# Two stages of a one-core kernel take a block of adaptive weights at every step instead of every second one

## The chip, the cores and the metric

The kernel runs on one core of a Trainium2 chip. The metric is the device time of one execution in microseconds (us). Before the change the median of 3 runs is 2345.33 us (2339.2 to 2347.9). The profile is of one execution of 2337.74 us, whose span is 2335.9 us.

## The reference

The model has two blocks over 256 tokens of width 1024. The change lies in the first one. There, for each of two layers, a vector of shifts, scales and gates is computed from the conditioning vector `c`, and it modulates what the mixer and the experts take in and give out:

```python
silu_c = jax.nn.silu(c)
for i in range(DEPTH):                                   # 2 layers
    mod = silu_c @ ada_w[i] + ada_b[i]                   # [1, 1024] @ [1024, 6144]
    sh_t, sc_t, ga_t, sh_c, sc_c, ga_c = jnp.split(mod, N_MOD, axis=-1)
    hn = modulate(rms_norm(x, norm_tm_g[i]), sh_t, sc_t)
    tm = rwkv7_mix(hn, ...) if i == 0 else dilated_attention_mix(hn, ...)
    x = x + ga_t[:, None, :] * tm
    hn = modulate(rms_norm(x, norm_cm_g[i]), sh_c, sc_c)
    x = x + ga_c[:, None, :] * hier_moe(hn, ...)
```

`ada_w` is 2 x 1024 x 6144 floats, 48 MB. Only `sh_t` and `sc_t` of layer 0 are needed before the first mixer, the recurrence (`rwkv7_mix`); the rest is needed after it. The second block (two layers of attention and experts) is not touched.

## The kernel before, in words

The products with `ada_w` are cut into six sections (`Ada.steps`, L1823 on): two layers times three stretches of 2048 columns. A section has 9 steps. Each of the first 8 loads one block of 128 x 2048 floats (1 MB, L78) into a tile `w` and does four matmuls with it (L1840; each shows as two rows in the trace, so a step is 8 rows), one per group of 32 columns of the array, all adding into one PSUM tile. The 9th step works on VectorE: it adds the bias `S` (L1843), for sections with a norm weight `G` scales with it (L1845), and puts the sum as two parts into `R` (L1848, L1850, L1848). `S` and `G` are loaded from the POOL queue (L1828, L1834).

The tiles `w` come from a pool of 4 slots (`nw=4`). `G` takes one of the same slots, and holds it until its section's 9th step has read it. The LoRA weights `lb` take another until the preparation's LoRA matmuls (L893) are done.

Section 0 runs at the start. The other five, 45 steps with 40 blocks, are the generator `side`, and are handed out as filler beside the recurrence's stages:

- `preps(1, ...)`, the second half of the recurrence's preparation (L866 to L950): it builds decays, keys and removal vectors on VectorE, ScalarE and GpSimd, with small matmuls between (L893, L924, L947). It gives 19 turns. `weave` (L581) takes one item of the filler per turn.
- `inverses()` (L993 to L1015): 16 transposes (L1000) bring 16 x 16 blocks to other partitions, 15 rounds of two VectorE instructions (L1006, L1008) invert them, each round needing the one before, and 16 transposes (L1013) bring them back. It gives 16 turns.
- the recurrence itself (L1235): two chains of 8 jobs each, forward and backward, go round in turn with `every(side, 3)`, one step per three rounds.

`every(gen, n)` (L595) takes one step of `gen` and lets n turns go per step. The instructions are then put in order by a list scheduler, so a step's load and its matmuls may stand somewhat before or after the turn that issued them; on each engine they run strictly in that order. After the recurrence comes the output projection with `rw_w_o` (L1257), whose weights go through the same 4 slots.

Of the kernel before, what the change touches and what calls it, by code (L numbers as in the profile page):

```python
# [575 lines left out]
def finish(gen):  # L576
    for _ in gen:
        pass


def weave(main, *fill, rest=True):  # L581

    fill = [iter(f) for f in fill]
    for _ in main:
        while fill:
            try:
                next(fill[0])
                break
            except StopIteration:
                fill.pop(0)  # L590
    for f in fill if rest else ():
        finish(f)


def every(gen, n):  # L595

    for _ in gen:
        for _ in range(n):
            yield
# [104 lines left out]
def rwkv(N, src, I, cst, emit, side, tail, scratch):  # L704
# [5 lines left out]
    def pool(name, bufs=1, st=es, side="right"):  # L710
        return st.enter_context(tc.tile_pool(name=N.nm(name), bufs=bufs, side=side, reuse_waits="tile"))
# [4 lines left out]
    en, e0, e1, e1a = (ExitStack() for _ in range(4))  # L716
# [104 lines left out]
    side = iter(side)  # L821
# [39 lines left out]
    def kknorm(u):  # L861
        sq = [scratch(k).rearrange("p (j t) -> p j t", j=2) for k in range(2)]
        for j in range(4):
            v.tensor_scalar(kn[:, 4 * u + j], kf[:, 4 * u + j], pv[:, 4, 4 * u + j:4 * u + j + 1], -1.0, op0=OP.mult, op1=OP.mult)
        for k in range(2):
            sc.activation(sq[k], kn[:, 4 * u + 2 * k:4 * u + 2 * k + 2], AF.Square)  # L866
        yield
        ps = N.psum("b")
        for j in range(4):
            nc.tensor.matmul(ps[0:8, :T], sel[:, j, :], sq[j // 2][:, j % 2], start=j == 0, stop=j == 3)  # L870
        ri = p2.tile([8, T], F32, tag="ri", name=N.nm("ri"))
        sc.activation(ri, ps[0:8, :T], AF.Sqrt)
        v.tensor_scalar(ri, ri, 1e-12, None, op0=OP.max)
        v.reciprocal(ri, ri)
        yield
        for j2 in range(2):
            ps = N.psum("b")
            for j in range(2):
                nc.tensor.matmul(ps[:, j * T:(j + 1) * T], selT[0:8, 2 * j2 + j, :], ri, start=True, stop=True)
            o = kn[:, 4 * u + 2 * j2:4 * u + 2 * j2 + 2]  # L880
            v.tensor_mul(o, o, ps.rearrange("p (j t) -> p j t", j=2))
        yield
# [69 lines left out]
    def pair(e2, q):  # L952
        live = [prep(z, e2, q) for z in range(2)]
        while live:
            for p in list(live):
                if next(p, live) is live:
                    live.remove(p)
            yield

    def preps(u, q, lag):  # L960
        yield from kknorm(u)
        a, b = pair(2 * u, q2), pair(2 * u + 1, q)
        for _ in range(lag):
            if next(a, b) is b:
                break
            yield
        roundrobin_ = [a, b]
        while roundrobin_:
            for p in list(roundrobin_):
                if next(p, b) is b:  # L970
                    roundrobin_.remove(p)
                yield
# [9 lines left out]
        for z in range(2):  # L982
            X[z] += [ry2.tile([P, 2, 512], F32, name=f"{n}{z}{e}") for e in range(2, 4)]

    weave(preps(1, pool("q3", 2, e0), 1), every(side, 2), rest=False)
    e0.close()
    e2s = ExitStack()
    p2 = pool("p2", 1, e2s)
# [4 lines left out]
    def inverses():  # L993
        g.memset(mcm, 0.0)
        for c in range(16):
            g.memset(mcm[:, c, :, c:c + 1], 1.0)
        for t4 in range(4):
            ps = N.psum("b")
            for t in range(4):
                nc.tensor.transpose(ps[0:64, t * P:(t + 1) * P], nd[:, 4 * t4 + t, :], N.ident)  # L1000
            sc.activation(ncm[:, 4 * t4:4 * t4 + 4].rearrange("p t b i -> p (t b i)"), ps[0:64, :], AF.Copy)
        yield
        for k in range(15, 0, -1):
            n = 16 - k
            tv = tmp[:, 0:n * 8 * k].rearrange("p (c b i) -> p c b i", c=n, b=8)
            v.tensor_mul(tv, ncm[:, k:k + 1, :, 0:k].to_broadcast([64, n, 8, k]),  # L1006
                         mcm[:, k:, :, k:k + 1].to_broadcast([64, n, 8, k]))
            v.tensor_add(mcm[:, k:, :, 0:k], mcm[:, k:, :, 0:k], tv)  # L1008
            yield
        for h in range(2):  # L1010
            ps = N.psum("b")
            for c in range(8):
                nc.tensor.transpose(ps[:, c * 64:(c + 1) * 64], mcm[:, 8 * h + c].rearrange("p b i -> p (b i)"),  # L1013
                                    N.ident[0:64, 0:64])
            sc.activation(m16[:, 8 * h:8 * h + 8], ps.rearrange("p (c x) -> p c x", c=8), AF.Copy)  # L1015
    m16 = pool("m16", 1, eM, "left").tile([P, 16, 64], F32, name="m16")
    weave(inverses(), every(side, 2), rest=False)
    e2s.close()
    en.close()

# [914 lines left out]
class Model:  # L1935
# [3 lines left out]
    def all(self):  # L1939
# [5 lines left out]
        with ExitStack() as es:  # L1945
# [28 lines left out]
            for i in range(2):  # L1974
# [11 lines left out]
                if i == 0:  # L1986
                    def side():
                        for q in range(1, 6):
                            yield from ada.steps(q // 3, q % 3)
                    mixer = rwkv(N, src, I, I["cst_rwkv"], emit, side(), tail, lambda k: half("G", k))  # L1990
                else:
                    mixer = dilated(N, src, I, I["cst_attn"], emit, tail)
# [186 lines left out]
```

## Time and profile before

| | us |
|---|---|
| median of 3 runs | 2345.33 |
| profiled execution | 2337.74, span 2335.9 |
| PE busy | 2038.8 (87% of the span) |
| VectorE (DVE) busy | 1097.0 (47%) |
| preparation, second half | about 180 to 239 |
| inverses (first L1000 to last L1013) | 239.2 to 264.0 |
| recurrence (first L1106 to last L1225) | 264.0 to 458.5 |

PE is TensorE's matmuls, PEld its weight loads, DVE VectorE, ACT ScalarE, POOL GpSimd, SP the queue that issues the loads of `w`. The end of a matmul is modelled, its start is measured, so the distance from start to start is the safer reading. PEclk is the share of full speed that TensorE's clock was granted: 0.50 is 1.2 GHz, 1.00 is 2.4 GHz. The chain that ended last reaches back only over the last 8 us of the program and says nothing of this place, so the stages are read from the timeline of each engine.

### The profile page before, as it was taken

Reading aid. Unit: us, or ns where it says so; the run is one execution under the profiler, and the core shown is the slowest. Engines: PE = TensorE matmul, PEld = TensorE weight load, DVE = VectorE, ACT = ScalarE, POOL = GpSimd, SP = SyncE. Lnnn points to the kernel's source line nnn. Section 1 sums busy time; section 2 is a strip of 40 time slices with the busy share of each in tenths; the row PEclk is TensorE's granted clock in tenths of the full one; section 3 lists DMA queues with packets and bytes.
Section 4 is the critical chain, followed back from the end, with each engine's and each line's share of the span. In section 5 each row is a group of like instructions: output and inputs, shape, how many; then the busy total and the mean of one; then the engine's idle time right before and its main releaser. Section 6 shows DMA issues by size and latency. Waiting matters only on the chain. (4 is left out here: it accounts for less than half of the span.)

```text
span 2335.9 us, 40948 instructions
## 1 busy us (share of the span) xinstructions
PE 2038.8 (87%) x16656; PEld 1459.6 (62%) x16656; DVE 1097.0 (47%) x2437; ACT 679.0 (29%) x1197; POOL 360.6 (15%) x296
## 2 busy tenths in 40 slices
PE   4987899979976999998987799979897799979886
PEld 2864577666543898986643577766563577756552
DVE  4777667663312435364321375562231765642222
ACT  2342133331112344442110245431120345421120
POOL 1144022220000321210000222220010222210010
PEclk7986799989988999999997799989998899989997
DMA  9434643578998553538999644479999443669996
GB/s 278 145 95 147 213 160 102 184 290 336 418 420 340 183 178 101 189 91 339 418 420 419 225 137 134 144 273 379 419 401 410 152 144 127 219 257 412 413 400 267
DMA packets 162999, 605.99 MB, mean 259 GB/s; under 512 B 36961, under 2 KB 37985, under 8 KB 107489
## 3 DMA queue, kind: packets, MB, share of 16 engines
q1 hardware_dynamic: 159072, 599.54, 67.7%
q0 software_dynamic: 3136, 3.16, 0.5%
q8 instruction: 139, 2.28, 0.4%
q14 instruction: 76, 0.61, 0.1%
q10 hardware_dynamic: 576, 0.39, 0.1%
HBM read 601.99 MB, written 1.05 MB: 258 GB/s over the span
## 5 line engine op out<-in xcount | busy, mean ns | idle before, releaser
L360 PE MATMUL psb<-w,xg 128*32 128x256 f32 (+1 forms) x4096 | 394.9, 432 | 87.9 <-DMA w<-in_moe_w_up_dram 27.1
L360 PEld LDWEIGHTS psb<-w,xg 128*32 128x32 f32 (+1 forms) x4096 | 213.4, 135 | 278.5 <-issue 70.7
L561 ACT ACTIVATE wh<-w 128x1024 fp32r<-128x1024 f32 x230 | 240.6, 1060 | 286.4 <-PE psb L651 147.9
L565 POOL TENSOR_TENSOR wl<-w,wh 128x1024 fp32r<-128x1024 f32 x80 | 197.9, 2475 | 577.4 <-ACT wh L561 457.0
L565 DVE TENSOR_TENSOR wl<-w,wh 128x1024 fp32r<-128x1024 f32 x150 | 200.6, 1344 | 166.8 <-ACT wh L561 138.8
L420 DVE SCALAR_TENSOR_TENSOR hid<-psb,gs,sg 128x256 f32<-128x256 f32 x44 | 30.0, 682 | 399.6 <-PE psb L360 399.6
L650 PE MATMUL psb<-wh,xh 128*128 128x512 f32 x448 | 184.8, 413 | 4.0 <-ACT wh L561 2.4
L651 PE MATMUL psb<-wh,xl 128*128 128x512 f32 x448 | 181.5, 406 | 0.3 <-DVE xl L143 0.3
L360 PE MATMUL psb<-w,hT 128*32 128x512 f32 (+1 forms) x1024 | 167.0, 597 | 6.3 <-DMA w<-in_moe_w_down_dram 2.9
L648 PE MATMUL psb<-wl,xh 128*128 128x512 f32 x448 | 130.2, 398 | 3.2 <-POOL wl L565 1.7
L142 ACT ACTIVATE yh<-psb 128x512 fp32r<-128x512 f32 x88 | 52.6, 597 | 228.5 <-DVE psb L441 126.8
L143 DVE TENSOR_TENSOR yl<-psb,yh 128x512 fp32r<-128x512 f32 x88 | 60.9, 692 | 99.7 <-ACT yh L142 99.7
L360 PE MATMUL psb<-pm,xh 128*128 128x256 f32 (+1 forms) x384 | 103.2, 304 | 4.3 <-DVE pm L343 4.3
L360 PEld LDWEIGHTS psb<-w,hT 128*32 128x32 f32 (+1 forms) x1024 | 46.0, 119 | 93.9 <-issue 74.2
L404 ACT ACTIVATE pt<-psb 128x256 fp32r<-128x256 f32 x44 | 16.9, 385 | 295.8 <-PE psb L360 295.8
L650 PEld LDWEIGHTS psb<-wh,xh 128*128 128x128 f32 x448 | 86.3, 193 | 24.2 <-ACT wh L561 3.6
L1840 PE MATMUL psb<-w,c_fm 128*32 128x512 f32 x384 | 75.4, 754 | 28.4 <-DMA w<-in_ada_w_dram 28.3
L648 PEld LDWEIGHTS psb<-wl,xh 128*128 128x128 f32 x448 | 85.2, 191 | 23.3 <-POOL wl L565 2.5
L360 PE MATMUL psb<-pm,xl 128*128 128x256 f32 (+1 forms) x384 | 99.4, 294 | 0.0
L651 PEld LDWEIGHTS psb<-wh,xl 128*128 128x128 f32 x448 | 86.7, 193 | 18.2 <-DVE xl L143 1.2
L619 PE MATMUL psb<-axh,wh 128*128 128x256 f32 x384 | 93.9, 283 | 0.0
L619 PE MATMUL psb<-axl,wh 128*128 128x256 f32 x384 | 93.9, 283 | 0.0
(577 smaller groups left out, 3751.4 us busy)
## 6 DMA issues: line engine op xcount, KB each, us to landing
w<-in_moe_w_gate_dram SPq DMA_DIRECT2D x64, 1024.0 KB, 18.0
w<-in_moe_w_up_dram SPq DMA_DIRECT2D x64, 1024.0 KB, 18.2
w<-in_moe_w_down_dram SPq DMA_DIRECT2D x64, 1024.0 KB, 19.8
w<-in_w_exp_up_dram SPq DMA_DIRECT2D x64, 1024.0 KB, 13.5
w<-in_w_exp_gate_dram SPq DMA_DIRECT2D x64, 1024.0 KB, 10.5
w<-in_w_exp_down_dram SPq DMA_DIRECT2D x64, 1024.0 KB, 16.5
w<-in_ada_w_dram SPq DMA_DIRECT2D x48, 1024.0 KB, 4.9
w<-in_w_in_dram SPq DMA_DIRECT2D x44, 1024.0 KB, 5.1
```

What stands on the lines that cost most here:

```text
L142: self.nc.scalar.activation(hi, src, AF.Copy)
L143: (eng or self.nc.vector).tensor_sub(lo, src, hi.bitcast(F32))
L360: keep(nc.tensor.matmul(*a, **k))
L404: nc.scalar.activation(pt[g], ps[:, 0:256], AF.Copy)
L420: v.scalar_tensor_tensor(hid[g].rearrange("s j p -> s p j"), pu[:, :256].rearrange("s (p j) -> s p j", j=2), gs[g], sg.rearrange("s (p j) ...
L561: nc.scalar.activation(wh, w, AF.Copy)
L565: i = (nc.gpsimd if eng == "g" else nc.vector).tensor_sub(wl, w, wh.bitcast(F32))
L619: mm = lambda a, b, **f: nc.tensor.matmul(o, a[:, kk, ws], b[:, k, :], skip_group_check=True, **f)
L648: nc.tensor.matmul(pss[tt], xh[:, k, t], wl[:, kk, :], start=False, stop=k == nk - 1)
L650: nc.tensor.matmul(pss[tt], xh[:, k, t], wh[:, kk, :], start=k == 0, stop=False)
L651: nc.tensor.matmul(pss[tt], xl[:, k, t], wh[:, kk, :], start=False, stop=False)
L1840: nc.tensor.matmul(ps[32 * j:32 * j + 32, :], self.c[:, k:k + 1].to_broadcast([P, 32]), wt[:, j * 512:(j + 1) * 512], start=k == 0, stop=k ...
```

## The change

In two of the three places one step of `side` is taken per turn, where one was taken per two turns:

```diff
-    weave(preps(1, pool("q3", 2, e0), 1), every(side, 2), rest=False)
+    weave(preps(1, pool("q3", 2, e0), 1), side, rest=False)
...
-    weave(inverses(), every(side, 2), rest=False)
+    weave(inverses(), side, rest=False)
```

The preparation's 19 turns give out 19 steps instead of 10, the inverses' 16 turns 16 instead of 8. The recurrence is left with 10 of the 45 steps instead of 27. No instruction is added or removed; steps are issued earlier. The order of the built programs shows where they come to stand.

TensorE's order from the end of the preparation to the first transposes of the inverses. Names with `w` are blocks, L947 is the preparation's last matmul group, L1000 the transposes. Before:

```order
L947 MATMUL psb_1714<-cm_252,aa_1491 128x4 x4
L947 MATMUL psb_1720<-cm_252,aa_1503 128x4
L1840 MATMUL psb_1734<-w_1735,c_fm 32x512
L947 MATMUL psb_1720<-cm_252,aa_1503 128x4 x3
L1840 MATMUL psb_1734<-w_1735,c_fm 32x512 x3
L1000 MATMUL psb_1772<-ident,nd 64x128 x4
```

And now:

```order
L1840 MATMUL psb_1634<-w_1747,c_fm 32x512 x4
L1096 MATMUL psc_2040<-vt,cm 128x128
L947 MATMUL psb_1759<-cm_252,aa_1503 128x4 x4
L1840 MATMUL psb_1634<-w_1753,c_fm 32x512 x4
L947 MATMUL psb_1765<-cm_252,aa_1515 128x4 x4
L1840 MATMUL psb_1634<-w_1771,c_fm 32x512 x4
L1840 MATMUL psb_1634<-w_1777,c_fm 32x512 x4
L1840 MATMUL psb_1792<-w_1793,c_fm 32x512 x4
L1000 MATMUL psb_1830<-ident,nd 64x128 x4
```

Three whole blocks, the last two of section 2 and the first of section 3, now stand directly ahead of the transposes L1000. Between the last L924 groups of the preparation (the first of them starts at 220.57 us before) and L1000 there are now seven blocks (w_1707 to w_1793), where there was one. Ahead of L1013 there are 25 of the 40 blocks, where there were 16.

TensorE's order in the first job of the recurrence, at the second level of the small solves (L1138 with the second `Mt`). Before:

```order
L1127 MATMUL psc_2077<-ident,MQB_1901 64x64 x8
L1166 MATMUL psc_2088<-ident,bk_843 128x128 x4
L1127 MATMUL psc_2094<-ident,MQB_1902 64x64 x8
L1138 MATMUL psb_2105<-Mt_2086,MQB_1901 64x32 x8
L1840 MATMUL psb_1960<-w_2145,c_fm 32x512
```

And now:

```order
L1127 MATMUL psc_2184<-ident,MQB_2010 64x64 x8
L1166 MATMUL psc_2195<-ident,bk_843 128x128 x4
L1127 MATMUL psc_2201<-ident,MQB_2011 64x64 x8
L1840 MATMUL psb_1919<-w_1960,c_fm 32x512 x4
L1840 MATMUL psb_1919<-w_1968,c_fm 32x512 x4
L1840 MATMUL psb_1919<-w_1976,c_fm 32x512 x4
L1840 MATMUL psb_2171<-w_2172,c_fm 32x512 x4
L1138 MATMUL psb_2212<-Mt_2193,MQB_2010 64x32 x8
```

Four blocks stand directly ahead of that L1138, where none did. From L1013 to this L1138 there are now eight blocks (w_1928 to w_2172), where there were two; after it seven are left, where there were 22.

VectorE's order in the preparation, where the 9th step of section 1 (`S_1410`) used to stand behind the last L949 but one. Now:

```order
L928 TENSOR_SCALAR cu_1489<-aa_1461,pv 128x256 x2
L1843 TENSOR_TENSOR S_1410<-S_1410,psb_1412 128x512
L930 SCALAR_TENSOR_TENSOR cu_1489<-cu_1489,kf 128x512
L1848 SCALAR_TENSOR_TENSOR R_127<-S_1410,arow,R_127 128x512
L914 TENSOR_TENSOR ar_1392<-kn,E_1552 128x512
L1850 TENSOR_TENSOR S_1410<-S_1410,R_127 128x512
L915 SCALAR_TENSOR_TENSOR bk_1396<-kn,aa_1503 128x512
L1848 SCALAR_TENSOR_TENSOR R_128<-S_1410,arow,R_128 128x512
```

Its four instructions stand in the middle of the preparation's own. Behind the recurrence, the last section's 9th step (L1843 to L1848) no longer stands in VectorE's order, and the first two splits of `rw_w_o` (L561, L565) stand about a third into the recurrence instead of behind it.

## Rows read from the trace of the kernel before

**Rows 1.** The page: busy tenths in 40 slices of 58.4 us.
```profile
PE   4987899979976999998987799979897799979886
DMA  9434643578998553538999644479999443669996
```

**Rows 2.** Windows, all: stretch, length, PE, PEld, DVE, ACT, POOL busy, PEclk, DMA, GB/s.
```profile
264.00:458.50 194.50, 193.12 (x4086) 149.76 (x4086) 124.74 (x344) 70.88 (x206) 45.66 (x76) 0.99 0.44 149
...
240.00:264.00 24.00, 14.89 (x90) 4.96 (x88) 18.96 (x33) 2.85 (x5) 3.52 (x6) 0.64 0.83 286
```

**Rows 3.** Windows, L1840 alone: stretch, length, PE, PEld busy, PEclk, DMA, GB/s.
```profile
264.00:458.50 194.50, 31.05 (x192) 4.45 (x192) 0.99 0.44 149
...
175.00:264.00 89.00, 29.95 (x128) 4.40 (x128) 0.65 0.49 173
```

**Rows 4.** Timeline of PE, 220 to 243: start, us, instruction [idle before <- releaser].
```profile
220.57 1.12 PE L924 MATMUL psc<-ar,bk 64*64 64x64 f32 x16 [7.39 <-DVE nm L935]
...
236.00 1.44 PE L947 MATMUL psb<-cm,aa 128*128 128x4 f32 x6
237.37 1.93 PE L1840 MATMUL psb<-w,c_fm 128*32 128x512 f32 x6
239.23 3.06 PE L1000 MATMUL psb<-ident,nd 128*64 128x128 f32 x16
```

**Rows 5.** Timeline of DVE, 233 to 262.
```profile
233.91 0.67 DVE L1843 TENSOR_TENSOR S<-S,psb 128x512 f32<-128x512 f32 x1
...
237.56 0.74 DVE L1848 SCALAR_TENSOR_TENSOR R<-S,arow,R 128x512 fp32r<-128x512 f32 x1
238.34 0.69 DVE L1850 TENSOR_TENSOR S<-S,R 128x512 f32<-128x512 f32 x1
...
243.07 0.28 DVE L1006 TENSOR_TENSOR tmp<-ncm,mcm 64x120 f32<-64x120 f32 x1 [3.25 <-ACT ncm L1001]
...
261.07 0.36 DVE L1008 TENSOR_TENSOR mcm<-mcm,tmp 64x120 f32<-64x120 f32 x1
```

**Rows 6.** Timeline of PE, 250 to 264.
```profile
250.79 1.94 PE L1840 MATMUL psb<-w,c_fm 128*32 128x512 f32 x8 [5.28 <-DMA w<-in_ada_w_dram]
253.26 1.93 PE L1840 MATMUL psb<-w,c_fm 128*32 128x512 f32 x8 [0.53 <-DMA w<-in_ada_w_dram]
...
262.19 1.86 PE L1013 MATMUL psb<-ident,mcm 64*128 64x64 f32 x15
```

**Rows 7.** Windows of 4 us, all, columns as in rows 2.
```profile
216.00:220.00 4.00, 0.00 (x0) 0.00 (x0) 4.00 (x5) 0.00 (x0) 1.80 (x2) 0.71 1.00 403
...
228.00:232.00 4.00, 1.98 (x9) 1.72 (x8) 4.00 (x10) 0.00 (x0) 3.31 (x3) 0.50 0.00 0
...
260.00:264.00 4.00, 3.68 (x27) 1.90 (x27) 3.00 (x5) 0.60 (x1) 0.81 (x2) 0.50 0.41 103
...
268.00:272.00 4.00, 4.00 (x68) 2.43 (x65) 3.18 (x7) 0.56 (x2) 0.34 (x1) 0.89 0.79 261
```

**Rows 8.** Loads of the tensor in_ada_w_dram: issue to landing, all 48.
```profile
DMA to landing us min/median/max: 4.6/4.9/14.7
```

**Rows 9.** Timeline of PE in the recurrence.
```profile
277.78 0.61 PE L1138 MATMUL psb<-Mt,MQB 64*64 64x32 f32 x16
...
289.30 1.06 PE L1840 MATMUL psb<-w,c_fm 128*32 128x512 f32 x8
290.30 0.45 PE L1211 MATMUL psc<-ident,YH 64*64 64x64 f32 x8
```

**Rows 10.** Timeline of DVE behind the recurrence.
```profile
459.31 0.68 DVE L1850 TENSOR_TENSOR S<-S,R 128x512 f32<-128x512 f32 x1
...
460.58 0.74 DVE L1848 SCALAR_TENSOR_TENSOR R<-S,arow,R 128x512 fp32r<-128x512 f32 x1
...
464.22 1.21 DVE L565 TENSOR_TENSOR wl<-w,wh 128x1024 fp32r<-128x1024 f32 x1
```

**Rows 11.** Timeline of PE behind the recurrence.
```profile
465.48 1.19 PE L648 MATMUL psb<-wl,oxh 128*128 128x512 f32 x4 [1.85 <-DVE wl L565]
```

## The prediction, as written before the changed kernel ran

> **What bounds the kernel now.** I read the page's 40 slices first [rows 1]: the change lies in slices 3 to 8, where the DMA engines are far from full while the experts' slices (9 to 12) are near 9. So I went on to windows of each stage and to the engines' timelines.
>
> In the second half of the preparation VectorE is the busy engine: between 216 and 220 us it is busy all 4.00 us and PE not at all, and between 228 and 232 us PE has 1.98 of 4 us [rows 7]. PE's L924 had stood 7.39 us for VectorE's L935 [rows 4]. PE has room there, and that is the room the change fills.
>
> In the inverses (239.2 to 264.0) the end is set by VectorE's 30 dependent instructions, 243.07 to 261.43 (261.07 + 0.36), that is 18.4 us [rows 5]. Beside them PE takes seven blocks and waits for each load: 5.28, then 0.53 us, with starts 2.47 us apart [rows 6]. DMA is at 0.83 there [rows 2]. So the loads are nearly level with VectorE's chain already, with no room for many more.
>
> In the recurrence PE is busy 193.12 of 194.5 us [rows 2], and a step of the filler stands in its row without a gap: from 289.30 to the next start at 290.30 is 1.00 us [rows 9]. The filler has 192 rows there, 24 blocks; before it 128 rows, 16 blocks [rows 3].
>
> **The change part by part.** The turns say that 17 steps leave the recurrence. The order says less: 16 blocks move to an earlier turn, but only 9 come ahead of L1013 (25 instead of 16), and seven stay at the head of the recurrence's first job. I go by the order.
>
> *Recurrence.* 24 blocks become 15 behind L1013, 9 x 1.00 = -9.0 us [rows 3, 9]. Bounds: -9.0, if PE is what the recurrence waits for; 0, if the small solves' chain through ScalarE and VectorE sets the pace and PE's row merely looks full. I take -9.0, since the trace shows no idle around the steps.
>
> The Trainium skill speaks against that (Perfetto Trace Analysis, Identifying the Most-Contended Engine): matmul busy time is not a good measure of TensorE's headroom, LDWEIGHTS busy is better. Here PEld is 149.76 of 194.5 us, 77% [rows 2]. By this rule PE has a quarter of headroom, the term could be 0, and the sum below would be +11.0. No trace here decides between them.
>
> *Preparation to L1000.* Seven blocks instead of one stand between the last L924 groups and L1000, six more. One costs 1.00 us at full clock [rows 9], and 1.93 at half [rows 6]: 6.0 to 11.6. PE's idle time there takes in 2.0 [rows 7]. To that comes a wait that was not there. Of the 4 slots, section 2's `G` holds one until VectorE has done that section's 9th step, and section 3's `G` takes another, so two are left for blocks when section 3 begins. Its first block w_1793 can be loaded only when w_1771's matmuls are done, and between the two on PE stands only w_1777. A load takes 4.9 us from issue to landing [rows 8]; less w_1777's own 1.0 to 1.9 that is 3.9 to 3.0 of waiting with L1000 queued behind it, and behind L1000 ScalarE's copies and VectorE's whole chain. Together 6.0 + 3.9 - 2.0 = 7.9 to 11.6 + 3.0 - 2.0 = 12.6. If VectorE's own delay covers part of it the lower bound is nearer 6. The clock decides: it was 0.50 from 228 to 232 us, with PE half idle, and 0.89 after PE had run without a break from 260 to 268 [rows 7]. PE's row from L924 on is now unbroken up to w_1793, so I take a value near the fast end, +8.5.
>
> Section 1's 9th step (0.67 + 0.74 + 0.69 + 0.74 = 2.8 us, rows 5) moves from VectorE's gap at 234 to 240 us into the middle of its full stretch. It delays the L941s behind which the L947s wait by 2.8 us, but the added blocks on PE run for longer beside it, so it adds nothing to the 8.5. Without that cover it would be the 2.8.
>
> *Inverses.* Eight blocks instead of seven stand ahead of L1013. From w_1793's landing: its matmuls 1.0 to 1.9, then 239.23 to 243.07 for L1000 and the copies, 3.8 [rows 4, 5], then 18.4: VectorE is done after 23.2 at the earliest. Eight loads at 2.47 us and the last one's matmuls: 19.8 + 1.9 = 21.7 [rows 6]. So VectorE's chain hides the loads with 1.5 us to spare: 0, bounds 0 and +3.
>
> The Trainium skill (DMA: Bandwidth & Descriptors, Bandwidth) has 6.15 us and 341 GB/s for a transfer of 1 MB. The rows have 4.9 us alone and 2.47 us apart, 424 GB/s [rows 6, 8]; the measurement decides. By the Trainium skill's figure the two waits of a single load would be 1.25 us longer each, the eight loads 24.6 + 1.9 = 26.5 us and so 3.3 late, and the sum +7.8.
>
> *First job of the recurrence.* Eight blocks instead of two stand between L1013 and the second L1138; their matmuls are in the 15. But w_1960, w_1968, w_1976 and w_2172 stand in one piece ahead of it, and w_2172 takes w_1968's slot: its load starts when w_1968 is done, so PE waits 4.9 - 1.0 = 3.9 us, with both chains of jobs queued behind. The 1 MB of `lg2` stands ahead of it on SP, at most 2.47 more: 6.4. Below, 0, if another slot is free by then. I take +4.5.
>
> *Behind the recurrence.* VectorE loses L1850 and L1848, 0.68 + 0.74, and one split of `rw_w_o`, 1.21 us, from a stretch with little idle [rows 10]; PE's 1.85 us of waiting for that split [rows 11] can go. All of it would be -4.5, but the norms of the last heads are next in line there, so I take -2.0; the other end is 0. No load behind it starts earlier that an end waits for: the experts' first loads still wait for the recurrence's memory.
>
> Sum: -9.0 + 8.5 + 0 + 4.5 - 2.0 = +2.0 us. The profiled execution took 2337.74 us, 7.6 below the median of its runs, so the sum gives 2339.7 for an execution like it and 2347.3 against the median, which is what I predict: 2347.
>
> **The rivals.**
>
> *The recurrence returns nothing (slower).* The place is the two chains of jobs: if Mt, ZZ and UW through ScalarE and VectorE set the pace, a removed block leaves a gap of 1.00 us. The sum is then +11.0, 2356; it decides as soon as less than about 7 of the 9 us come back. For it: PEld is at 77% only [rows 2]. Against it: PE's starts abut around the block [rows 9], and PE is idle 1.4 us in the whole stretch. By the Trainium skill's rule above this rival would be the likelier one.
>
> *The clock stays down (slower).* Loads of 2.47 us with 1.93 us of matmuls kept the clock at 0.50 through the inverses [rows 6, 7]. The seven blocks left over carry this pattern into the first job; before, the clock was up in the window from 268 us on. If PE works at half clock up to the second L1138, the 9.8 us from 268 to 277.78 [rows 7, 9], 0.89 of them at full clock, take about 9 more: +11, 2356. It decides if PE waits for loads between L1106 and w_1952. Against it: those loads have a lead, as VectorE's chain holds PE before L1013.
>
> *No new wait (faster).* If L1000 waits for no load and its six steps fit into PE's gaps, and w_2172 lands in time: -9.0 - 4.5 = -13.5, 2332. The preparation's idle PE and DMA engines speak for it, the count of slots against it.
>
> *Nothing moves in effect.* The blocks are issued earlier, but loads and slots hold them to about the old pace, and what is lost ahead of the recurrence is exactly what is saved in it: 0, 2345.
>
> **How the numbers follow.** The forecast has 0.58 (its own range -4 to +9, 2341 to 2354), the recurrence that returns nothing 0.13, the low clock 0.12, no new wait 0.08, nothing 0.09. All bounds together go from 6.0 - 9.0 - 4.5 = -7.5 to 12.6 + 3 + 6.4 = +22. I give 2335 to 2361. What a measurement of this kernel can tell from no change is about 0.5%, 11.7 us. Faster than that is almost only the third rival: 0.08. Slower takes half of the first two and the forecast's upper end: 0.13 x 0.45 + 0.12 x 0.5 + 0.58 x 0.08 = 0.16. Same: 0.76.
>
> **What would show it.** After the change L1000 should start at 246 to 251 us, behind a PE wait of 3 to 4 us for a load; L1006 to L1008 should still take 18.4; L1013 should end 6 to 12 us later than 264.0. In the first job PE should wait some 4 us for w_2172's load, and the second L1138 start near 297 (277.8 + 8.5 + six steps of 1.00 + 4.5). From there to the last L1225 it should take 15 us less than the 180.7 before, with 7 blocks. I am wrong if L1000 starts before 243, if that stretch shortens by less than 8 us, or if the total moves by more than 12 us.

## The result: 0.9% slower, and the profile after

The changed kernel takes 2363.69 us (median of 6 runs, 2357.25 to 2368.5), the kernel before 2340.32 us (median of 6 runs, three of them those given above the change). The ratio is 1.0089, with a 95% interval of 1.0076 to 1.0103: about 21 us more, where 2 were predicted. It lies above the stated range of 2335 to 2361.

The profiled execution is the slowest of its runs, 2368.5 us, 28 us above the median of before. So I account for it only up to the first L343, the first instruction behind the first routing of tokens to experts: 516.0 us before, 540.5 after. That is +24.5, close to the difference of the medians.

The page's slices after, to be held against [rows 1]. The DMA engines are now nearly idle in slices 7 and 8 (the digits 2 and 0), since the filler has run out there; TensorE's clock has dropped in slices 5 and 6, from the digits 7 and 9 before to 6 and 8.

```profile
PE   4988789988987799998997799979897799979885
PEclk7986689998998899998998789989998899989997
DMA  9425852066999652528999734478999534579996
```

Windows, all engines, one for each stage: second part of the preparation to the first L1000, inverses, first job to the first L1191, rest of the recurrence to the first L1255, output projection to the first L343. Columns as in [rows 2]. First the kernel before:

```profile
216.00:239.20 23.20, 15.72 (x108) 11.57 (x108) 20.23 (x44) 0.00 (x0) 6.74 (x21) 0.54 0.25 102
239.20:264.00 24.80, 15.69 (x95) 5.62 (x92) 19.58 (x34) 2.85 (x5) 3.52 (x6) 0.64 0.81 276
264.00:283.60 19.60, 19.60 (x359) 14.70 (x358) 9.46 (x20) 5.26 (x13) 0.70 (x1) 0.88 0.69 236
283.60:458.50 174.90, 173.52 (x3733) 135.05 (x3730) 115.28 (x324) 65.62 (x193) 44.96 (x75) 1.00 0.41 139
458.50:516.00 57.50, 43.58 (x191) 33.59 (x188) 42.48 (x95) 20.52 (x33) 17.09 (x10) 0.87 0.82 309
```

Then the changed kernel:

```profile
216.00:255.10 39.10, 30.25 (x172) 13.42 (x172) 25.31 (x51) 0.00 (x0) 10.70 (x26) 0.53 0.67 243
255.10:283.40 28.30, 18.10 (x100) 5.98 (x96) 19.59 (x35) 2.96 (x5) 1.16 (x3) 0.68 0.96 344
283.40:324.20 40.80, 31.20 (x406) 17.52 (x406) 11.00 (x21) 5.25 (x13) 3.27 (x6) 0.76 0.78 259
324.20:486.20 162.00, 155.54 (x3616) 133.01 (x3613) 109.75 (x318) 68.13 (x195) 49.03 (x73) 0.99 0.20 64
486.20:540.50 54.30, 43.15 (x191) 33.60 (x189) 38.09 (x91) 18.87 (x31) 15.41 (x9) 0.86 0.84 312
```

Stage by stage the lengths differ by +15.9, +3.5, +21.2, -12.9 and -3.2: +24.5. The recurrence gives back 12.9 of the 15.0 us that it was to give back; the three stages ahead of it take 40.6, three times as much.

The timeline of PE in the preparation, which answers to [rows 4]. In brackets stands how long PE was idle before an instruction, and what ended it:

```profile
217.56 1.58 PE L1840 MATMUL psb<-w,c_fm 128*32 128x512 f32 x8 [3.48 <-DMA w<-in_ada_w_dram]
...
224.98 1.12 PE L924 MATMUL psc<-ar,bk 64*64 64x64 f32 x16 [3.10 <-DVE nm L935]
...
227.35 1.93 PE L1840 MATMUL psb<-w,c_fm 128*32 128x512 f32 x8
...
244.62 1.87 PE L947 MATMUL psb<-cm,aa 128*128 128x4 f32 x8
246.43 3.64 PE L1840 MATMUL psb<-w,c_fm 128*32 128x512 f32 x16
253.24 1.93 PE L1840 MATMUL psb<-w,c_fm 128*32 128x512 f32 x8 [3.17 <-DMA w<-in_ada_w_dram]
255.11 3.62 PE L1000 MATMUL psb<-ident,nd 128*64 128x128 f32 x16
```

The wait for w_1793 is there as predicted, 3.17 us. Two other things were not. First, the L924 that waits for VectorE's L935 starts at 224.98 instead of 220.57 [rows 4], 4.4 us later: section 1's 9th step now stands ahead of that L935 on VectorE (four instructions, 2.84 us), which also waited 1.23 us for ScalarE at 206.48. Second, the clock did not rise. From 227.35 to 250.07 PE's row is without a gap (the timeline shows no idle time between these lines either), and yet the blocks in it take 1.8 to 1.9 us instead of 1.06. The granted clock of the whole stretch is 0.53, as it was 0.54 before. There are eight more blocks in it than before (172 against 108 instructions, eight to a block), and PE's busy time grew by 14.5 us.

The timeline of PE in the inverses, which answers to [rows 6]:

```profile
269.64 1.93 PE L1840 MATMUL psb<-w,c_fm 128*32 128x512 f32 x8 [1.18 <-DMA w<-in_ada_w_dram]
272.13 1.93 PE L1840 MATMUL psb<-w,c_fm 128*32 128x512 f32 x8 [0.56 <-DMA w<-in_ada_w_dram]
274.62 1.72 PE L1840 MATMUL psb<-w,c_fm 128*32 128x512 f32 x8 [0.56 <-DMA w<-in_ada_w_dram]
277.11 1.06 PE L1840 MATMUL psb<-w,c_fm 128*32 128x512 f32 x8 [0.76 <-DMA w<-in_ada_w_dram]
279.69 1.93 PE L1840 MATMUL psb<-w,c_fm 128*32 128x512 f32 x8 [1.52 <-DMA w<-in_ada_w_dram]
281.55 1.97 PE L1013 MATMUL psb<-ident,mcm 64*128 64x64 f32 x16
```

And VectorE's chain beside it, the first and the last of 30, which answers to [rows 5]:

```profile
259.46 0.28 DVE L1006 TENSOR_TENSOR tmp<-ncm,mcm 64x120 f32<-64x120 f32 x1 [5.62 <-ACT ncm L1001]
...
276.12 0.35 DVE L1008 TENSOR_TENSOR mcm<-mcm,tmp 64x120 f32<-64x120 f32 x1
```

VectorE is done at 276.47, but two blocks still stand ahead of L1013, and the blocks come no faster than one per 2.49 to 2.58 us. DMA is at 0.96. The end of this stage has passed from VectorE to the loads.

The timeline of PE in the first job:

```profile
303.34 1.06 PE L1840 MATMUL psb<-w,c_fm 128*32 128x512 f32 x8 [1.44 <-DMA w<-in_ada_w_dram]
312.24 1.93 PE L1840 MATMUL psb<-w,c_fm 128*32 128x512 f32 x8 [7.84 <-DMA w<-in_ada_w_dram]
314.11 1.92 PE L1138 MATMUL psb<-Mt,MQB 64*64 64x32 f32 x32
...
321.50 2.95 PE L1172 MATMUL psb<-AW,MQB 64*64 64x128 f32 x30
```

PE waits 7.84 us for w_2172 and comes back at half clock: the second-level L1138, 1.07 us for 32 elsewhere, takes 1.92. It starts at 314.11 instead of 277.78 [rows 9]. Up to 306 us the clock was at 0.94; from 306 to 312 PE stood idle, and from 312 to 324 it was busy 11.76 of 12 us at 0.51. The load that it waited for is the first of these two on SP:

```profile
301.97 2.83 SPq L78 DMA_DIRECT2D w<-in_ada_w_dram  x2
```

It was issued when w_1968 was done (301.90), as predicted, but PE waited for it until 312.24, that is 10.3 us after its issue, where a load was taken to need 4.9 [rows 8]. Two more transfers of 1 MB were under way beside it, `lg2` from 297.33 and the next block from 304.5.

Behind the recurrence the first split of `rw_w_o` is now there in time. PE, which answers to [rows 11]:

```profile
487.56 0.73 PE L650 MATMUL psb<-wh,oxh 128*128 128x512 f32 x2 [0.31 <-ACT oxh L142]
...
489.86 1.07 PE L648 MATMUL psb<-wl,oxh 128*128 128x512 f32 x4
```

The 1.85 us before L648 are gone; on VectorE only the norms and the later splits are left of [rows 10].

### The profile page after: what moved, and what is told of

Read it like the earlier page. It is cut to its first block, busy times and chain, and to the rows that moved or that the text cites. A ratio compares the mean times of both kernels' runs of the same rounds, so it can differ in the third digit from the quotient of the medians.

```text
span 2366.6 us, 40956 instructions
## 1 busy us (share of the span) xinstructions
PE 2056.3 (87%) x16656; PEld 1466.2 (62%) x16656; DVE 1092.4 (46%) x2437; ACT 679.7 (29%) x1197; POOL 364.9 (15%) x296
## 5 line engine op out<-in xcount | busy, mean ns | idle before, releaser
L561 ACT ACTIVATE wh<-w 128x1024 fp32r<-128x1024 f32 x230 | 240.5, 1060 | 289.1 <-PE psb L651 149.2
L565 POOL TENSOR_TENSOR wl<-w,wh 128x1024 fp32r<-128x1024 f32 x80 | 198.7, 2485 | 588.4 <-ACT wh L561 467.7
L565 DVE TENSOR_TENSOR wl<-w,wh 128x1024 fp32r<-128x1024 f32 x150 | 200.5, 1343 | 167.2 <-ACT wh L561 139.0
L648 PE MATMUL psb<-wl,xh 128*128 128x512 f32 x448 | 129.9, 397 | 3.3 <-POOL wl L565 1.7
L1840 PE MATMUL psb<-w,c_fm 128*32 128x512 f32 x384 | 81.8, 866 | 46.6 <-DMA w<-in_ada_w_dram 46.6
L648 PEld LDWEIGHTS psb<-wl,xh 128*128 128x128 f32 x448 | 84.8, 191 | 23.3 <-POOL wl L565 2.6
```

The source lines that it names most:

```text
L561: nc.scalar.activation(wh, w, AF.Copy)
L565: i = (nc.gpsimd if eng == "g" else nc.vector).tensor_sub(wl, w, wh.bitcast(F32))
L648: nc.tensor.matmul(pss[tt], xh[:, k, t], wl[:, kk, :], start=False, stop=k == nk - 1)
L1840: nc.tensor.matmul(ps[32 * j:32 * j + 32, :], self.c[:, k:k + 1].to_broadcast([P, 32]), wt[:, j * 512:(j + 1) * 512], start=k == 0, stop=k ...
```

## The experiments

Fourteen kernels were run. Ratios are to the runs of the kernel before on the same chip (medians 2342 to 2344 us; 2340.32 for the changed kernel). The columns behind are starts in the profiled execution, in us. Each is from one execution, and that of the changed kernel is its slowest, 4.8 us above its median, so the columns can show a gain over it larger than the medians do.

| kernel | median | ratio, interval | first L1000 | first L1106 | first L1191 | first L1255 | first L343 |
|---|---|---|---|---|---|---|---|
| before | 2340.32 | 1 | 239.2 | 264.0 | 283.6 | 458.5 | 516.0 |
| changed | 2363.69 | 1.0089 (1.0076 to 1.0103) | 255.1 | 283.4 | 324.2 | 486.2 | 540.5 |
| preps_only | 2344.85 | 1.0005 (0.9991 to 1.0019) | 254.3 | 278.3 | 299.2 | 466.1 | 516.3 |
| inv_only | 2362.13 | 1.0072 (1.0048 to 1.0096) | 239.2 | 269.0 | 306.6 | 483.4 | 537.2 |
| slot_g | 2357.44 | 1.0063 (1.0039 to 1.0087) | 246.3 | 274.6 | 312.7 | 474.2 | 526.2 |
| no_loads | 2336.94 | 0.9969 (0.9957 to 0.9981) | 241.5 | 272.8 | 290.7 | 450.0 | 503.1 |
| half_loads | 2338.42 | 0.9987 (0.9972 to 1.0003) | 242.0 | 273.8 | 296.1 | 459.3 | 512.0 |
| before_no_loads | 2350.9 | 1.0037 (1.0021 to 1.0053) | 239.1 | 265.6 | 285.1 | 461.0 | 517.7 |
| before_slot_g | 2343.43 | 1.0003 (0.9991 to 1.0015) | 238.7 | 264.7 | 283.7 | 460.7 | 516.1 |
| preps_slot_g | 2342.21 | 0.9998 (0.9985 to 1.0010) | 252.2 | 277.1 | 298.0 | 466.1 | 518.9 |
| hot | 2350.84 | 1.0039 (1.0026 to 1.0052) | 248.9 | 275.6 | 306.4 | 468.4 | 518.5 |
| hot_slot_g | 2347.35 | 1.0025 (1.0007 to 1.0042) | 245.4 | 273.7 | 305.0 | 466.3 | 517.7 |
| early | 2343.55 | 1.0006 (0.9991 to 1.0021) | 240.0 | 266.0 | 286.6 | 462.6 | 512.8 |
| preps_hot | 2337.86 | 0.9982 (0.9965 to 0.9999) | 246.4 | 271.7 | 291.2 | 458.6 | 508.8 |
| before_hot | 2346.18 | 1.0016 (0.9999 to 1.0032) | 241.4 | 265.2 | 285.4 | 460.4 | 516.1 |
| recurrence_bare | 3068.36 | 1.3100 (1.3068 to 1.3132) | 237.7 | 262.3 | 281.3 | 430.3 | 480.5 |

Where a kernel computes other values, tokens go to other experts, and what follows the routing is other work: recurrence_bare moved 882 MB instead of 606 MB. Of no_loads, half_loads, before_no_loads and recurrence_bare I therefore use the columns up to L343, not the median, and hold their expectations against these.

**One stage alone.** preps_only and inv_only have one of the two lines of the change each.

> Only the preparation takes a block at every step; the inverses keep every second. Theory A (waits for loads in TensorE's row, made by too few slots): L1000 starts near 255 as with both, the inverses end near 280 and the first job waits for no load; 9 fewer steps in the recurrence return 0.85 us each. +16 - 8 = +8 us, about 2348. Theory B (the recurrence returns nothing, the delay is all there is): +16, about 2356.

> Only the inverses take a block at every step. Theory A: L1000 stays at 239, but sixteen steps ask for loads at twice the pace, L1013 and the second L1138 wait for them: +15 to +20 there, 8 fewer steps in the recurrence return 7, so about +10, 2350. Theory B (the preparation alone is to blame, the loads in the inverses lie under VectorE's chain): -7, about 2333.

The preparation alone comes out even; the inverses alone carry the loss, and neither theory had that: preps_only came out better than both, inv_only worse. Up to L1191 the two add up to nearly the whole: 15.6 and 23.0 us late, against 40.6 with both lines. preps_only gets 8.0 back in the recurrence, as its theory A said, and 7.3 behind it, which neither theory had; what earns the 7.3 there was not traced. inv_only gets back nothing in the recurrence: 176.8 us against 174.9, with seven blocks fewer. Windows of inv_only, all:

```profile
269.00:306.60 37.60, 31.76 (x403) 17.82 (x404) 11.49 (x22) 5.25 (x13) 1.85 (x4) 0.77 0.94 322
306.60:483.40 176.80, 168.49 (x3681) 137.37 (x3678) 116.07 (x322) 67.84 (x195) 50.17 (x75) 0.97 0.31 102
```

PE's busy time did fall, by 5.0 us, but its idle time rose from 1.4 to 8.3. The waits of PE there (what waited for what; us, times, longest):

```profile
PE psb L1106 <- ACT YH L1196: 6.0, 6, 2.9
```

In the kernel before this wait is 0.9 us. The longest one, in the timeline of VectorE and PE of inv_only:

```profile
427.88 0.73 DVE L1848 SCALAR_TENSOR_TENSOR R<-S,arow,R 128x512 fp32r<-128x512 f32 x1
...
430.71 2.84 DVE L1252 TENSOR_TENSOR ar<-ar,ar 128x512 f32<-128x512 f32 x1
...
433.47 0.74 DVE L1848 SCALAR_TENSOR_TENSOR R<-S,arow,R 128x512 fp32r<-128x512 f32 x1
434.13 0.28 DVE L1194 TENSOR_TENSOR RA<-psc,ar 128x128 f32<-128x128 f32 x1
...
435.54 0.44 PE L1106 MATMUL psb<-ar,bk 64*64 64x128 f32 x4 [2.92 <-ACT YH L1196]
```

A section's 9th step and the head of the output projection stand in VectorE's order ahead of L1194, which both chains of jobs wait for. The other five waits I did not trace.

**Without the bytes.**

```diff
-            wt = N.wload(w[:, k, s * 2048:(s + 1) * 2048])
+            if (i, s) != (0, 0):          # no_loads, before_no_loads
+                if not hasattr(self, "one"):
+                    self.one = N.wload(w[:, k, s * 2048:(s + 1) * 2048])
+                wt = self.one
...
+            wt = N.wload(w[:, k, s * 2048:s * 2048 + 2048 // hf])   # half_loads, hf = 2
```

> The changed kernel with the loads of sections 1 to 5 left out but for the first: every later block's matmuls read that one tile (the values are not the reference's). Theory A (the waits for loads are the cost): the second L1138 starts near 293 instead of 314, the recurrence returns its 13 us, total about 24 us less than the changed kernel, near 2340. Rival D (the added matmuls in TensorE's row at the low clock are the cost): at most 5 us less, near 2359.

> The changed kernel in which every block of sections 1 to 5 loads half of its 2048 columns (0.5 MB instead of 1 MB) and uses that half twice, so that the gates' values are not the reference's; matmuls, slots and order as in the changed kernel. Theory A (the changed kernel asks for 1 MB per step faster than the DMA engines bring it: in the inverses its blocks stood 2.5 us apart): with half the bytes the waits at blocks all but go, 2336 to 2344, the idle time before blocks falls from 62 us to under 25. Theory B (the waits come from the slots and from the order in which they free, and from the half clock, not from bytes): 2354 to 2364, idle time before blocks over 45 us.

> The kernel before with the blocks of sections 1 to 5 all reading one tile, the loads left out (values not the reference's). It prices the waits for loads that the kernel before already has (28.5 us of idle time before blocks between 180 and 340 us). Theory A (with loads left out it makes no difference at which step a block stands, since the work of the blocks is the same): 2333 to 2341, as with the changed kernel without loads (2337), so that the waits of before were worth 3 to 11 us. Theory B (blocks at every step have a price of their own beside their loads, or the recurrence does not return what it is spared): under 2330, clearly faster than the changed kernel without loads.

With the loads left out of both kernels the change gains 517.7 - 503.1 = 14.6 us at L343 (the rival *no new wait* had put it at 13.5), and by L1191 it is late by only 5.6 (290.7 against 285.1). So the blocks' own work on PE is cheap; with the loads goes the rest, 35.0 of the 40.6 us (waits, and the half clock that came with them). In no_loads theory A held and rival D fell, but more came back than theory A's 24 us: 37.4 at L343. Half the bytes, with slots and order as in the changed kernel, take L343 from 540.5 to 512.0. That speaks for the bytes, but it doesn't part them from the clock, which rose with it to 0.66 in the preparation and 0.84 in the inverses (0.53 and 0.68 in the changed kernel). The waits did not all but go: PE and its weight loads still stood 44.9 us before blocks (62.4 in the changed kernel), but in 31 pieces instead of 24. That count of theory A failed; its time held, read at L343 (4.0 us ahead of the kernel before).

before_no_loads is not faster than before up to L343 (+1.7), and 14.6 us behind no_loads, so neither of its theories held. The waits that the kernel before already has (PE 10.7 us between 180 and 340 us) cost it nothing that can be seen; that VectorE's chain ends later there anyway would explain it.

**Slots.**

```diff
-            G = N.wp.tile([P, 2048], F32, name=N.nm("G"), tag="w")[:, 0:512]
+            G = N.gpool.tile([P, 512], F32, name=N.nm("G"), tag="Gs")
```

> The changed kernel with the norm weights G in a small tile of their own, so that all 4 slots hold blocks. Theory A (slots): the first block of section 3 can be loaded one block earlier, L1000 starts 3 us earlier (252), fewer waits in the inverses and in the first job, in all 6 to 12 us faster than the changed kernel, 2352 to 2358. Rival C (DMA throughput or the clock set the pace, not slots): unchanged, 2362 to 2365.

> The kernel before with G, the norm's weights (which hold one of the four load slots in sections 2 and 3 until the section ends), in a small tile of its own, so that four slots serve blocks. Theory A (slots limit the loads in the kernel before as in the changed one, where this gave 6 us): 2337 to 2341. Theory B (at every second step three slots are enough): 2343 to 2346.

> Blocks at every step of the preparation, at every second of the inverses, and G in a tile of its own. Theory A (blocks in the preparation alone came out even, 2344.9, since the waits at their loads ate what the recurrence returned, and with four slots these waits shrink by 6 to 9 us): 2335 to 2340, faster than the kernel before. Theory B (the preparation is bound by the bytes of its loads, or by the half clock, so a fourth slot gives nothing): 2343 to 2346.

A fourth slot brings L1000 8.8 us forward in the changed kernel and 6 us in the median (theory A of slot_g). The inverses stay as long as without it, 28.3 us. At every second step it brings nothing, and with blocks at every step of the preparation alone too little to be told from no change (theory B for before_slot_g, and nearer to B for preps_slot_g, where L1000 came only 2.1 us earlier).

**The clock.**

```diff
+            if k and 1 <= 3 * i + s <= 4:
+                for j in range(4):
+                    nc.tensor.matmul(ps[32 * j:32 * j + 32, :], self.z.to_broadcast([P, 32]),
+                                     N.ident[:, None, :].to_broadcast([P, 4, P]), start=False, stop=False)
```

> The changed kernel in which, in sections 1 to 4, TensorE runs in front of each block but a section's first one more pass of the block's size (4 column groups of 512) with a column of zeros, which adds nothing to the sums; it can run while the block's load is awaited. It tells how much of the cost is the half clock behind the waits. Theory A (the loads' bytes set the pace, TensorE's clock matters little): the time stays within 6 us of the changed kernel, 2358 to 2370, whatever the clock does. Theory B (the half clock from 220 to 285 us and at 314 us is what costs, and the added passes lift it): granted clock above 0.9 there and 2345 to 2355.

> The changed kernel with both: the added zero passes in sections 1 to 4 and G in a tile of its own. Theory A (half clock and slots are two costs, 13 us and 6 us of the 22, and the rest is the bytes of the loads in the inverses): they add up, 2343 to 2347, level with the kernel before. Theory B (both shorten the same waits, so they overlap): 2348 to 2352.

> The kernel before with the zero passes in sections 1 and 2, which it takes ahead of the recurrence at every second step. Its granted clock is 0.50 to 0.7 from 216 to 264 us as well. Theory A (there VectorE's chain ends last, so TensorE's clock costs nothing): 2341 to 2346. Theory B (the half clock costs in the kernel before too): 2332 to 2339.

Work that adds nothing makes the changed kernel 12 to 13 us faster (theory B of hot). Windows of hot, all:

```profile
216.00:248.90 32.90, 24.52 (x228) 9.85 (x228) 23.27 (x48) 0.00 (x0) 8.66 (x23) 0.92 0.83 291
248.90:275.60 26.70, 20.22 (x164) 6.87 (x160) 19.52 (x35) 2.50 (x5) 2.31 (x5) 0.91 1.00 357
275.60:306.40 30.80, 30.36 (x458) 16.58 (x456) 10.77 (x21) 5.41 (x14) 1.89 (x3) 1.00 0.92 315
```

The clock is at 0.92, 0.91 and 1.00 instead of 0.53, 0.68 and 0.76, and L1191 comes 17.8 us earlier. The Trainium skill (TensorE: Matmul & The Clock Gate, Part 1) says that the low clock is the resting state and that activity lifts it; this run agrees. But PE's busy time does not tell the two levels apart. The same 20 us, all, first of the changed kernel, then of hot:

```profile
220.00:240.00 20.00, 16.69 (x114) 8.16 (x114) 16.19 (x38) 0.00 (x0) 5.31 (x5) 0.50 0.56 188
220.00:240.00 20.00, 17.70 (x196) 8.67 (x196) 15.70 (x38) 0.00 (x0) 6.38 (x21) 1.00 0.79 274
```

PE is busy 16.69 us at 0.50 in the one and 17.70 us at 1.00 in the other. What in the zero passes lifts the clock stays open. In the inverses PE's blocks keep their distance though:

```profile
258.02 1.06 PE L1846 MATMUL psb<-w,c_fm 128*32 128x512 f32 x8 [2.08 <-DMA w<-in_ada_w_dram]
...
260.50 1.06 PE L1846 MATMUL psb<-w,c_fm 128*32 128x512 f32 x8 [0.55 <-DMA w<-in_ada_w_dram]
...
263.00 1.06 PE L1846 MATMUL psb<-w,c_fm 128*32 128x512 f32 x8 [0.58 <-DMA w<-in_ada_w_dram]
```

2.48 and 2.50 us at full clock, with the DMA engines at 1.00: there the clock does not set the distance, and with four slots as well (hot_slot_g) the stage is no shorter, 28.3 us. What is left is the bytes, and half_loads fits: there such blocks came 1.26 to 1.84 us apart. Lifting the clock takes 22.0 us off at L343 and halving the bytes 28.5, together twice what was lost; so the two are not separate shares of the loss, and either takes half of it or more away. Clock and slot together leave 0.25% over the kernel before, and L1191 at 305.0. In the medians the two nearly add up (11.7 and 6.1 us off, 15.0 together, each by its ratio), in this profile they overlap; which it is stays open. before_hot shows that the kernel before had nothing to gain in the inverses: the clock was at 0.86 there instead of 0.64, and from L1000 to L1191 it took 44.0 us instead of 44.4. For its preparation it shows nothing, since the clock stayed at 0.50 from 216 us to L1000 in spite of the passes.

**The recurrence, and a start in another place.**

> The kernel before without sections 3 to 5 of the adaptive weights (24 blocks, their loads, matmuls and sums; values not the reference's), so that nothing runs between the steps of the recurrence. It prices the blocks there. Theory A (TensorE is the bound of the recurrence and a block costs 0.86 to 1.0 us): recurrence 20 to 24 us shorter, 2316 to 2324. Theory B (what blocks at full rate in the inverses alone showed: the recurrence's own waits come in where a block leaves, so half or less comes back): 2328 to 2340.

> The kernel before, with the blocks started earlier: once the projections of the first half's preparation are through, its last steps take a block each, while the DMA engines are busy for only 0.24 of the time (150 to 190 us); every second step behind that, as before. 5 blocks more stand ahead of the recurrence. Theory A (what costs in the change is the bytes of the loads in a stretch where the DMA engines are full, and moving blocks to a stretch where they idle returns 0.86 us each): 2336 to 2340. Theory B (a block ahead of the recurrence costs TensorE's half-clock time there, 1.9 us, about what it returns): 2341 to 2347.

Without blocks the recurrence (L1106 to L1255) takes 168.0 us instead of 194.5: 26.5 for 24 blocks, 1.10 each with their share of the 9th steps, above theory A's 20 to 24. early gained 3.2 us at L343 in its profile, which the times don't bear out: from no change it can't be told, and 2343.55 lies where theory B put it.

**A version from the parts.** Blocks at every step of the preparation, every second in the inverses, `G` apart, zero passes in sections 1 to 3:

> Blocks at every step of the preparation, at every second of the inverses, G in a tile of its own, and the zero passes in sections 1 to 3. Theory A (in the preparation the half clock is what makes blocks dear; without it the 8 blocks taken out of the recurrence are nearly all gain): 2332 to 2338, faster than the kernel before. Theory B (the preparation is as long as its loads' bytes make it, whatever the clock): 2340 to 2344, as without the passes (2342).

It takes 2337.86 us, ratio 0.9982 (0.9965 to 0.9999): inside theory A's 2332 to 2338. Of the kernels that compute the whole reference it is the only one whose interval lies below 1, and by less than the 0.5% that can safely be told. Its windows, the recurrence and what follows:

```profile
291.20:458.60 167.40, 163.05 (x3669) 133.03 (x3666) 113.89 (x322) 67.71 (x195) 48.00 (x74) 1.00 0.31 102
458.60:508.80 50.20, 39.93 (x191) 31.25 (x189) 38.18 (x92) 18.86 (x31) 14.83 (x9) 0.93 0.88 320
```

By L1191 it is 7.6 us late, the recurrence returns 7.5, and the 7.3 behind it are the gain. So theory A had the time but only half the reason: slot and clock together halve the delay of preps_only (15.6), which is what lets the same 7.3 show; which of the two does it wasn't parted.

## Why the prediction was wrong

The direction of each term was right but the inverses', and the sum was 22 us short. Term by term, at L343:

| term | predicted | measured |
|---|---|---|
| preparation to L1000 | +8.5 | +15.9 |
| inverses | 0 | +3.5 |
| first job, to L1191 (wait 4.5 and six steps of 1.00) | +10.5 | +21.2 |
| recurrence behind it (15 blocks) | -15.0 | -12.9 |
| output projection | -2.0 | -3.2 |
| sum | +2.0 | +24.5 |

*Preparation.* This is the step that failed first: "PE's row from L924 on is now unbroken up to w_1793, so I take a value near the fast end". The row was unbroken, from 227.35 to 250.07, and the clock stayed at 0.50 all the same, so an unbroken row did not give the full clock. The trace of the kernel before could have warned; columns as in [rows 7]:

```profile
224.00:228.00 4.00, 4.00 (x45) 3.80 (x44) 4.00 (x11) 0.00 (x0) 0.89 (x1) 0.50 0.03 6
236.00:240.00 4.00, 4.00 (x17) 2.21 (x17) 2.27 (x4) 0.00 (x0) 0.00 (x0) 0.50 0.00 0
```

PE was busy all 4.00 us in both, at 0.50. From that L924 to L1000 it now takes 30.1 us instead of 18.7, +11.5, which is the prediction's own sum at half clock (11.6 + 3.0 - 2.0 = 12.6) within 1.1. The other 4.4 us are VectorE's delay, a term that it put at nothing: section 1's 9th step (2.84 of the 4.4), which "adds nothing to the 8.5". L924 itself waits for VectorE, so that delay adds to what PE does behind it and is not covered by it. With the clock lifted, hot has L1000 at 248.9, inside the predicted 246 to 251; but there L924 also starts at 221.60, so hot does not part the two.

*Inverses.* "So VectorE's chain hides the loads with 1.5 us to spare" held for two of its three numbers: from the L1006 to the last L1008 it took 17.0 us, and the blocks came 2.49 to 2.58 us apart. But 68 rows of blocks, eight and a half, stood in the stage, and two of them had waited 3.97 and 1.66 us first, so the loads ended 5 us behind the chain. The upper bound, 3, was just passed. no_loads shows the chain ending last again.

*First job.* w_2172's wait was named, at 3.9 to 6.4 us; it was 7.84, since its load took 10.3 us with two others under way. In all PE stood idle for 9.6 us of this stage where 4.5 were predicted, and it was busy for 11.6 us more where six steps of 1.00 were. Six blocks at 1.06 are 6.4 of these; most of the other 5.2 goes with the half clock from 312 to 324, behind the wait, a term that the sum put at nothing. The rival *the clock stays down* said this for the first job, at +11 us and a chance of 0.12. The measured excess there is 10.7, but its condition (waits between L1106 and w_1952) is not what happened: up to 306 us the clock was 0.94, and it fell in the wait for w_2172. Nor was the clock at 0.50 through the inverses, as that rival has it: 0.64 was their mean [rows 2]. That its number fits is luck, since half of the excess is waiting. hot, with the clock at 1.00, still needs 30.8 us for the stage, 6.25 of them zero passes.

*Recurrence.* The rival *returns nothing* fell. 48 rows of blocks instead of 168 stand behind L1191, 15 blocks less, and gave back 12.9 us, 0.86 each: PE's busy time fell by 18.0 and its idle time rose by 5.1, to 6.5, of which 4.0 are waits for `YH`. By the Trainium skill's rule (Perfetto Trace Analysis, Identifying the Most-Contended Engine) the quarter of headroom in PEld would have let the term be 0; here a block is worth 0.86 to 1.10 us whatever PEld says, and the measurement decides. But inv_only shows the other side of it in the same kernel: where the 9th steps fall on a bad place, seven blocks give back nothing.

*Load times.* The Trainium skill's 6.15 us for 1 MB (DMA: Bandwidth & Descriptors, Bandwidth) was measured there on transfers issued from GpSimd, while these are issued from SP. It would have made w_1793's wait 4.25 to 5.15 us; 3.17 was measured, and the blocks came at 406 to 421 GB/s. The sum by its figure, +7.8, comes nearer to 24.5 only by chance: the missing 22 us are the clock, VectorE's delay and loads that are under way together.

*Chances.* I gave "slower by over 0.5%" 0.16. Both the cost of the clock and that of the loads were on the list, as separate accidents with a chance each. They were not separate: in the first job the wait and the half clock behind it came together, and in the preparation the half clock was there from 227.35 on without a wait in the row. The prediction's own bounds added up to +22, near what was measured; the range was closed at 2361, +16.

*Its signs.* L1000 came at 255.1 (246 to 251 was said), behind a wait of 3.17 us (3 to 4). L1013 ended 19.5 us later than before (6 to 12), and the second L1138 started at 314.1 (297). From there to the last L1225 it took 8.6 us less (15); the mark for being wrong was 8. The total moved by more than 12 us, which was named as a sign of being wrong.

## What to carry to other kernels

Filler that reads 1 MB per step is paid at the rate of its bytes, here 2.5 us per step: before moving it to a stretch, set its bytes per microsecond there against what the DMA engines have left, not PE's idle time. Take TensorE's clock for the moved work from the granted clock that the rows of that stretch show before the change (0.54 here), not from how unbroken PE's row will look. Work added to an engine ahead of something that another engine waits for is not hidden by more work on that other engine; it adds (2.8 of the 4.4 us here). A stage whose end another engine's chain sets can take filler only until the loads end with that chain; here the stage then ended 5 us behind it.

## What was not expected of the hardware

- PE's row was without a gap for 22.7 us (227.35 to 250.07) at a granted clock of 0.50.
- One pass of zeros per block in front of the waits raised the granted clock from 0.53 to 0.92 in the preparation and made the whole kernel 12 to 13 us faster, though the zero passes kept PE busy for 37.1 us between 180 and 340 us.
- Half the bytes per load did not halve the distance of the blocks everywhere: it was 1.26 to 1.84 us where the loads followed each other, against 2.5.
- The weights' loads (1 MB) between 216 and 300 us took 7.5 us at the median from issue to landing, against 5.2 in the same stretch of the kernel before (4.9 over its whole run [rows 8]). The load that PE waited for in the first job took 10.3 us.
